# Issue order of the side work in the gate and up product of a SwiGLU layer: chunk loads and stores queued behind the unit loads

## The chip, the cores and the metric

The kernel runs on one core of one Trainium2 chip. Its time is the device time of one execution in microseconds. Three runs of the kernel before took 1671.94, 1673.28 and 1673.4 us; the median is 1673.28 us. The core's engines are called PE (matrix products), DVE (vector), ACT (scalar activation), POOL (GpSimd) and SP. SP computes nothing here: every transfer of this kernel is issued by SP, one after the other, and a transfer whose condition is not met holds all those written behind it.

## The reference, cut to what matters

One decoder layer with S = 1024 tokens and D = 1024 channels, all in float32. The first half (attention groups, a convolution branch, gates, an output projection, a LayerNorm) is not touched by the change. The second half is

```
def swiglu_ffn(x, w_gate, w_up, w_down):
    return (jax.nn.silu(x @ w_gate) * (x @ w_up)) @ w_down

x = layer_norm(alpha * x + swiglu_ffn(x, w_gate, w_up, w_down), ln2_g, ln2_b)
```

with 2816 hidden channels, 22 tiles of 128.

## The kernel before, in words

Each float32 product is made of three products of rounded halves: a matrix is split into `wh` (rounded, written by ACT, line 68) and `wl` (the rest, written by DVE, line 69), and PE adds `wh*xh + wl*xh + wh*xl`. On top of that the feed-forward uses a scheme with seven instead of eight half-size products (Strassen and Winograd), so sums of weight blocks and of activation blocks are needed.

**The tile loop** (`for f in range(NFF)`, line 1040). Tile f computes 128 hidden channels for all tokens. From tile 3 on it holds seven products of 12 matmuls, 84 in all; tiles 0 to 2 have 60, two products having been made early. The order on PE is B11 and B21 (gate), T2, T3, T1, then T4 (`t<-a22h` or `s<-a22h` in the trace), then B22. T4 is added into the same bank as T3, so PE may start it only when DVE has read T3's result (line 1072, `dve.tensor_add(u3, u2, pd)`).

**The weight units.** Each tile needs a gate unit g and an up unit u, 512 KB each, loaded by `fetch` (line 81, `raw<-wst`). While PE works on tile f, DVE and ACT prepare the weights of tile f+1: line 880 and 881 (`second`) form sums of u and g, line 885 and a split on ACT and DVE (`third`), then `fourth` and `fifth` (line 897). The two kinds of unit have separate pools: three buffers for g (`wraw`), two for u (`up2`). DVE runs its instructions in their written order, and line 880 for tile f+1 stands ahead of line 1072 for tile f.

**The chunks.** The down product, which follows the loop, also needs sums of its weights. They are made on the side in 22 chunks by `down_weights` (line 970): two loads of 256 KB (`tw<-wst`, lines 978 and 979), four POOL operations (lines 982 to 985) and, deferred to the next turn of the loop through the list `after`, two stores of 256 KB (`twd<-tw`, lines 988 and 989). Three buffers (`stage`) hold them. The loop text asks for one chunk in each tile from tile 3 on, and two in tiles 5, 9 and 13.

**The activation sums.** After each odd tile POOL forms four sums of the hidden activations (`down_sums`, lines 964 to 967, `h<-h`). Plain rows are stored at a tile's end (lines 1094, 1097 and 1098, `hdA<-h`), the sums through `after` (line 959, `hdS<-h`).

**What sets the order.** A scheduler places the instructions of each engine by when it reckons them ready, not by the order of the text. A chunk load depends on nothing but a free buffer, so the scheduler may put it far ahead of the place where the text has it.

Of the kernel before, what the change touches and what calls it, by code (L numbers as in the profile page):

```python
# [23 lines left out]
NEARLY = 3  # L24
# [17 lines left out]
def hybrid_layer(ctx: ExitStack, tc, wst, xT, xr, cosT, sinT, mask2, mask1, identc, convp, lnrows, out):  # L42
    nc = tc.nc
    pe, act, dve, sp = nc.tensor, nc.scalar, nc.vector, nc.sync
# [26 lines left out]
    state = {"raw": 0, "split": 0, "due": 0.0}  # L71
# [5 lines left out]
    def fetch(upto):  # L77
        while state["raw"] < min(upto, n_units):
            u = state["raw"]
            t = unit_pool[0](u).tile([P, 1024], F32, tag="raw", name="raw")  # L80
            sp.dma_start(t, wst[u])
            raws[u] = t
            state["raw"] += 1

    def prepare(upto):
        while state["split"] < min(upto, n_units):
            u = state["split"]
            fetch(u + 1)
            hi = wsplit.tile([P, 1024], F32R, tag="wh", name="wh")
            lo = wsplit.tile([P, 1024], F32R, tag="wl", name="wl")  # L90
            split(raws.pop(u), hi, lo)
            splits[u] = (hi, lo)
            state["split"] += 1
            fetch(u + 4)
# [11 lines left out]
    def take_into(w):  # L106
        u = taken[0]
        assert state["split"] == u
        taken[0] += 1
        fetch(u + 1)  # L110
        split(raws.pop(u), *w)
        state["split"] += 1
        fetch(u + 4)
        return w
# [788 lines left out]
    def product(ps, w, x, start=True, stop=True):  # L903
        n = 0
        for k in range(4):
            for a, b in three((w[0][:, k, :], w[1][:, k, :]), (x[0][:, k, :], x[1][:, k, :])):
                pe.matmul(ps, a, b, start=start and n == 0, stop=stop and n == 11,  # L907
                          skip_group_check=True)
                n += 1

    def bank(tag):
        return psum.tile([P, HALF], F32, tag=tag, name=tag)
# [8 lines left out]
    for n in range(NEARLY):  # L921
        t = stage.tile([P, S], F32, tag="sp", name="early")
# [27 lines left out]
    def half_tile():  # L950
        return gt6.tile([P, HALF], F32, tag="t", name="t")

    def row_tile():
        return h4.tile([P, S], F32, tag="h", name="h")
# [6 lines left out]
    def down_sums(k, u, v):  # L961

        eng = nc.gpsimd
        eng.tensor_add(v[:, RIGHT], v[:, RIGHT], u[:, RIGHT])
        eng.tensor_sub(u[:, RIGHT], u[:, LEFT], u[:, RIGHT])
        eng.tensor_sub(u[:, LEFT], v[:, RIGHT], u[:, LEFT])
        eng.tensor_sub(v[:, LEFT], v[:, LEFT], u[:, LEFT])
        after.append(lambda: spill_sums(k, u, v))

    def down_weights(k, e):  # L970

        t = stage.tile([P, 4, 256], F32, tag="sp", name="tw")
        cols = slice(e * 256, (e + 1) * 256)

        def rows(src, n):
            return src[n].rearrange("p (c x) -> p c x", c=2)[:, :, cols]

        sp.dma_start(t[:, 0:2], rows(wst, n_units + k))
        sp.dma_start(t[:, 2:4], rows(wst, n_units + NK + k))
        b11, b12, b21, b22 = (t[:, n] for n in range(4))  # L980
        eng = nc.gpsimd
        eng.tensor_sub(b12, b22, b12)
        eng.tensor_add(b11, b12, b11)
        eng.tensor_sub(b21, b21, b11)
        eng.tensor_sub(b22, b22, b11)  # L985

        def spill():
            sp.dma_start(rows(twd, k), t[:, 0:2])
            sp.dma_start(rows(twd, NK + k), t[:, 2:4])
        after.append(spill)  # L990

    chunks = deque((k, e) for k in range(NK) for e in range(2))
# [18 lines left out]
    def load_upto(n):  # L1011
        while dpos[0] < min(n, len(seq)):
            j, k = seq[dpos[0]]
            _, a, (kind, half), _, _ = DOWN[j]
            t = row_tile() if dpos[0] % 7 < 4 else wraw.tile([P, S], F32, tag="raw", name="raw")
            cols = slice(half * HALF, (half + 1) * HALF)
            b = wst[n_units + kind * NK + k] if kind < 2 else twd[(kind - 2) * NK + k]
            sp.dma_start(t[:, LEFT], hd[a][k])
            sp.dma_start(t[:, RIGHT], b[:, cols])
            draw[j, k] = t  # L1020
            dpos[0] += 1
# [12 lines left out]
    def start_down():  # L1034
        split_upto((0, 0), 1)
# [4 lines left out]
    for f in range(NFF):  # L1040
        last = f == NFF - 1
        todo, after = after, []
        for fn in todo:
            fn()
        if f >= NEARLY:
            for _ in range(2 if f in (5, 9, 13) else 1):
                if chunks:
                    down_weights(*chunks.popleft())
        V_, W = W, Weights()
        ta, tb_, tc_, td = sets[f % 2]  # L1050
        nxt = None if last else W
        if f < NEARLY:
            u2, sg1 = early[f]
            if nxt:
                nxt.first(f + 1 >= NEARLY)
        else:
            u2, sg1 = half_tile(), half_tile()
            pa = bank(ta)
            product(pa, V_.B11, A11, stop=False)
            act.activation(u2, pa, AF.Copy)  # L1060
            if nxt:
                nxt.first(f + 1 >= NEARLY)
        pb = bank(tb_)
        product(pb, V_.T2, S2)
        dve.tensor_add(u2, u2, pb)
        if f >= NEARLY:
            product(pa, V_.B21, A12, start=False)
            act.activation(sg1, pa, AF.Silu)
        u3, sg2 = half_tile(), half_tile()
        pd = bank(td)  # L1070
        product(pd, V_.T3, S3, stop=False)
        dve.tensor_add(u3, u2, pd)
        if last:
            load_upto(4)
        pc = bank(tc_)
        product(pc, V_.T1, S1, stop=False)
        dve.tensor_add(u3, u3, pc)
        if nxt:
            nxt.second()
        product(pd, V_.T4, a22, start=False)  # L1080
        dve.tensor_add(sg2, u2, pd)
        act.activation(sg2, sg2, AF.Silu)
        if nxt:
            nxt.third()
        else:
            start_down()
        product(pc, V_.B22, S4, start=False)
        dve.tensor_add(u2, u2, pc)
        ht = row_tile()
        dve.tensor_mul(ht[:, LEFT], sg1, u2)  # L1090
        dve.tensor_mul(ht[:, RIGHT], sg2, u3)
        k = FFN_ORDER[f] % NK
        if f % 2 == 0:
            sp.dma_start(hd["A11"][k], ht[:, LEFT])
            hrows.append(ht)
        else:
            sp.dma_start(hd["A12"][k], ht[:, LEFT])
            sp.dma_start(hd["A22"][k], ht[:, RIGHT])
            down_sums(k, hrows.pop(), ht)
        if nxt:  # L1100
            nxt.fourth()
            nxt.fifth()
# [203 lines left out]
```

## Time and profile before

| | before |
|---|---|
| median of three runs | 1673.28 us |
| the profiled execution | 1669.85 us |
| its span | 1668.0 us |
| PE busy | 1614.5 us, 97% of the span |
| DVE, ACT, POOL busy | 1034.5, 684.9, 161.9 us |
| mean granted TensorE clock | 0.984 |

The span is the stretch in which instructions ran; 1.85 us of the profiled execution lie around it. Times inside the span are counted from its start. The tile loop reaches from about 970 to 1449 us. A busy time is no proof that an engine is at its best: a matmul of this kernel is shown as 389 ns long, while the next one starts 227 ns after it, so the distance of starts is the measure. A granted clock of 1.0 is full speed, 2.4 GHz; half of it is 1.2 GHz.

### The profile page before, as it was taken

To read this page: it belongs to the slowest core of one execution; us is meant where nothing else is said; L and a number is where in the kernel's file an instruction comes from. 1 tells how busy PE (TensorE), PEld (TensorE's weight loads), DVE (VectorE), ACT (ScalarE), POOL (GpSimd) and SP (SyncE) were. 2 spreads that over 40 slices of the span, in tenths; PEclk is the share of its full clock that TensorE was granted. 3 is DMA by queue.
4 is the path that set the end of the run, shared out by engine and by line. 5 is a ranking of instruction groups with operands and counts; after the bars stand their busy time and mean duration, and the time that the engine had idled before them with its cause. 6 is when DMAs were issued, how large, how long until landed. Compare 5 with 4: busy or idle time off the path is not lost. (4 is left out here: it accounts for less than half of the span.)

```text
span 1668.0 us, 21325 instructions
## 1 busy us (share of the span) xinstructions
PE 1614.5 (97%) x8014; PEld 1316.0 (79%) x8014; DVE 1034.5 (62%) x1605; ACT 684.9 (41%) x1241; POOL 161.9 (10%) x148
## 2 busy tenths in 40 slices
PE   9999999999999999999999989867899999999998
PEld 7887788777887888887888868656788888888886
DVE  6944476553856942488756787454656666557685
ACT  5267743676345674334221142122232322344451
POOL 0000000000000000000000223555411112100000
PEclk9999999999999999999999999978999999999999
DMA  7111114111251124376725023766522332586761
GB/s 259 60 42 51 45 58 164 38 46 39 73 164 39 51 79 153 127 229 205 255 83 227 38 98 130 235 206 213 184 95 95 104 111 102 214 315 215 231 210 51
DMA packets 110812, 222.54 MB, mean 133 GB/s; under 512 B 14556, under 2 KB 39516, under 8 KB 110708
## 3 DMA queue, kind: packets, MB, share of 16 engines
q1 hardware_dynamic: 110708, 221.17, 39.4%
q8 instruction: 63, 1.03, 0.3%
q14 instruction: 41, 0.34, 0.1%
HBM read 159.81 MB, written 61.31 MB: 133 GB/s over the span
## 5 line engine op out<-in xcount | busy, mean ns | idle before, releaser
L68 ACT ACTIVATE wh<-raw 128x1024 fp32r<-128x1024 f32 (+1 forms) x192 | 192.4, 1002 | 442.2 <-PE mm L180 83.1
L69 DVE TENSOR_TENSOR wl<-raw,wh 128x1024 fp32r<-128x1024 f32 (+1 forms) x192 | 227.9, 1188 | 184.8 <-ACT wh L68 183.5
L180 PE MATMUL mm<-xh,wh 128*128 128x512 f32 x752 | 298.5, 397 | 0.0
L180 PE MATMUL mm<-xl,wh 128*128 128x512 f32 x752 | 293.2, 390 | 0.0
L180 PE MATMUL mm<-xh,wl 128*128 128x512 f32 x752 | 293.2, 390 | 0.0
L180 PEld LDWEIGHTS mm<-xh,wh 128*128 128x128 f32 x752 | 141.1, 188 | 39.3 <-issue 9.9
L180 PEld LDWEIGHTS mm<-xh,wl 128*128 128x128 f32 x752 | 141.2, 188 | 29.9
L180 PEld LDWEIGHTS mm<-xl,wh 128*128 128x128 f32 x752 | 141.3, 188 | 27.7
L508 DVE SCALAR_TENSOR_TENSOR acc<-u,cp,acc 128x1024 f32<-128x1024 f32 x120 | 153.9, 1282 | 3.3
L351 ACT ACTIVATE sw<-mm 32x512 f32<-32x512 f32 x192 | 113.3, 590 | 34.9 <-PE mm L180 16.5
L796 POOL TENSOR_TENSOR y<-y 128x512 f32<-128x512 f32 x3 | 6.5, 2167 | 956.9 <-DVE sc L618 947.6
L180 PE MATMUL mm<-wh,xh 128*128 128x512 f32 x232 | 91.5, 394 | 0.0
L180 PE MATMUL mm<-wh,xl 128*128 128x512 f32 x232 | 90.4, 390 | 0.0
L180 PE MATMUL mm<-wl,xh 128*128 128x512 f32 x232 | 90.3, 389 | 0.0
L353 DVE TENSOR_TENSOR tcs<-mm,cosF 128x512 f32<-128x512 f32 x48 | 33.2, 691 | 85.4 <-ACT sw L351 80.5
L69 DVE TENSOR_TENSOR wl<-h,wh 128x1024 fp32r<-128x1024 f32 x41 | 50.6, 1235 | 33.7 <-ACT wh L68 32.1
L68 ACT ACTIVATE wh<-h 128x1024 fp32r<-128x1024 f32 x41 | 43.5, 1061 | 63.7 <-PE s L1201 26.4
L382 DVE CUSTOM_DVE_ANT_0 pt<-s,m2t 128x256 f32<-128x256 f32 (+1 forms) x128 | 41.3, 378 | 35.4 <-PE s L418 35.4
L384 ACT ACTIVATE pt<-pt,stp 128x64 f32<-128x64 f32 (+2 forms) x128 | 49.9, 392 | 27.1 <-DVE stp L382 26.9
L907 PE MATMUL mm<-xh,wh 128*128 128x512 f32 x140 | 55.5, 398 | 4.4 <-ACT xh L785 4.4
L880 DVE TENSOR_TENSOR raw<-raw 128x512 f32<-128x512 f32 x22 | 16.6, 755 | 63.4 <-DMA raw<-wst 63.4
L907 PE MATMUL mm<-xl,wh 128*128 128x512 f32 x140 | 55.4, 396 | 0.0
(383 smaller groups left out, 3367.3 us busy)
## 6 DMA issues: line engine op xcount, KB each, us to landing
raw<-wst SPq DMA_DIRECT2D x121, 512.0 KB, 3.7
tw<-wst SPq DMA_DIRECT2D x44, 256.0 KB, 4.2
twd<-tw SPq DMA_DIRECT2D x44, 256.0 KB, 2.5
hdS<-h SPq DMA_DIRECT2D x44, 256.0 KB, 2.0
hdA<-h SPq DMA_DIRECT2D x33, 256.0 KB, 3.1
gd<-gt SPq DMA_DIRECT2D x16, 512.0 KB, 3.5
m<-gd SPq DMA_DIRECT2D x32, 256.0 KB, 5.1
h<-twd SPq DMA_DIRECT2D x25, 256.0 KB, 4.1
```

The lines of the kernel that those rows point to most:

```text
L68: act.activation(hi, src, AF.Copy)
L69: dve.tensor_sub(lo, src, hi.bitcast(F32))
L180: pe.matmul(ps, a, b, start=j == 0, stop=j == n - 1)
L351: act.activation(sw[32 * q:32 * q + 32, :], ps[32 * (q ^ 1):32 * (q ^ 1) + 32, :], AF.Copy)
L353: dve.tensor_mul(tcs, ps, cosF[:, cols])
L382: dve.tensor_tensor_reduce(out=pt, in0=s, in1=msk, scale=-0.125, scalar=BIG, op0=ALU.add, op1=ALU.min, accum_out=mneg)
L384: act.activation(pt, pt, AF.Exp, bias=mneg, scale=-1.0, accum_out=den)
L508: dve.scalar_tensor_tensor(acc, u[:, j:j + S], cp[:, c, j:j + 1], acc, op0=ALU.mult, op1=ALU.add)
L796: eng.tensor_add(v[:, RIGHT], v[:, RIGHT], v[:, LEFT])
L880: dve.tensor_sub(u[:, LEFT], u[:, RIGHT], u[:, LEFT])
L907: pe.matmul(ps, a, b, start=start and n == 0, stop=stop and n == 11, skip_group_check=True)
```

## The change

`fetch` keeps the instruction of the unit load that it issued last. In each turn of the tile loop, what the turn issues on SP of the deferred stores (`twd<-tw`, `hdS<-h`) and of the chunk loads (`tw<-wst`) is put behind that load in SP's order. This is a rule on the order of issue; no wait for the load's completion is added. Computation, sizes and buffers stay as they are. Lines behind 1042 have a number one higher in the changed kernel.

```
@@ -78,7 +78,7 @@
         while state["raw"] < min(upto, n_units):
             u = state["raw"]
             t = unit_pool[0](u).tile([P, 1024], F32, tag="raw", name="raw")
-            sp.dma_start(t, wst[u])
+            state["load"] = sp.dma_start(t, wst[u]).ins
             raws[u] = t
             state["raw"] += 1
 
@@ -1040,12 +1040,13 @@
     for f in range(NFF):
         last = f == NFF - 1
         todo, after = after, []
-        for fn in todo:
-            fn()
-        if f >= NEARLY:
-            for _ in range(2 if f in (5, 9, 13) else 1):
-                if chunks:
-                    down_weights(*chunks.popleft())
+        with tc.issue_after(state["load"]):
+            for fn in todo:
+                fn()
+            if f >= NEARLY:
+                for _ in range(2 if f in (5, 9, 13) else 1):
+                    if chunks:
+                        down_weights(*chunks.popleft())
         V_, W = W, Weights()
         ta, tb_, tc_, td = sets[f % 2]
         nxt = None if last else W
```

The order of instructions is the same on PE and on ACT. On DVE lines 880 and 885 change places in two tiles. SP and POOL change throughout the loop.

SP in tiles 2 and 3, before (`hdA_1_96` is the store at the end of tile 2; the second `raw` load is the u unit that tile 3 prepares for tile 4):

```order
L989 DMA twd_183<-tw 256x1x256
L978 DMA tw<-wst 128x2x256
L979 DMA tw<-wst 128x2x256
L978 DMA tw<-wst 128x2x256
L81 DMA raw<-wst 128x1024
L979 DMA tw<-wst 128x2x256
L988 DMA twd_173<-tw 256x1x256
L81 DMA raw<-wst 128x1024
L989 DMA twd_184<-tw 256x1x256
L1094 DMA hdA_1_96<-h 128x512
L988 DMA twd_173<-tw 256x1x256
```

The same place after:

```order
L81 DMA raw<-wst 128x1024 x2
L978 DMA tw<-wst 128x2x256
L1095 DMA hdA_1_96<-h 128x512
L979 DMA tw<-wst 128x2x256
L81 DMA raw<-wst 128x1024 x2
L1099 DMA hdA_1_118<-h 128x512
L1098 DMA hdA_1_107<-h 128x512
L988 DMA twd_172<-tw 256x1x256
L989 DMA twd_183<-tw 256x1x256
L959 DMA hdS_1_129<-h 128x512
```

Before, the chunk of rows 173 and 184, the third one, stands around the two unit loads, and a store that waits for POOL is directly ahead of the second. After, the two unit loads come as a pair ahead of the first chunk, and that chunk's stores stand behind the next pair. From there to the end of the loop one or two chunks stand between two pairs.

POOL at the same place, before, from the end of the second chunk on (each number names one buffer; `tw_8617` is the second chunk, `tw_8754` the third, `h_8346` and `h_8251` the activations of tiles 0 and 1):

```order
L985 TENSOR_TENSOR tw_8617<-tw_8617 128x256
L964 TENSOR_TENSOR h_8346<-h_8346,h_8251 128x512
L965 TENSOR_TENSOR h_8251<-h_8251 128x512
L966 TENSOR_TENSOR h_8251<-h_8346,h_8251 128x512
L967 TENSOR_TENSOR h_8346<-h_8346,h_8251 128x512
L982 TENSOR_TENSOR tw_8754<-tw_8754 128x256
```

and after (`tw_8471` is the first chunk, `h_8589` and `h_8454` the activations of tiles 2 and 3):

```order
L985 TENSOR_TENSOR tw_8471<-tw_8471 128x256
L964 TENSOR_TENSOR h_8589<-h_8589,h_8454 128x512
L965 TENSOR_TENSOR h_8454<-h_8454 128x512
L966 TENSOR_TENSOR h_8454<-h_8589,h_8454 128x512
L967 TENSOR_TENSOR h_8589<-h_8589,h_8454 128x512
L982 TENSOR_TENSOR tw_8617<-tw_8617 128x256
```

Before, two chunks stand ahead of the sums of tiles 0 and 1, and seven follow before the next sums. After, one chunk stands ahead of the sums of tiles 2 and 3, and three follow.

SP at the end of the loop, before (`hdA_9_104` is the store at the end of tile 18; `hdA_5_100` and the `wst` behind it are the sixth unit of the down product):

```order
L81 DMA raw<-wst 128x1024
L1094 DMA hdA_9_104<-h 128x512
L1018 DMA raw<-hdA_5_100 128x512
L1019 DMA raw<-wst 128x512
L1098 DMA hdA_9_126<-h 128x512
```

and after, where the sixth unit comes behind two more stores:

```order
L1095 DMA hdA_9_104<-h 128x512
L989 DMA twd_192<-tw 256x1x256
L978 DMA tw<-wst 128x2x256
L979 DMA tw<-wst 128x2x256
L978 DMA tw<-wst 128x2x256
L979 DMA tw<-wst 128x2x256
L978 DMA tw<-wst 128x2x256
L988 DMA twd_181<-tw 256x1x256
L989 DMA twd_192<-tw 256x1x256
L988 DMA twd_182<-tw 256x1x256
L989 DMA twd_193<-tw 256x1x256
L979 DMA tw<-wst 128x2x256
```

The last three chunks stand together there, between tile 18's store and the sixth unit of the down product.

## Rows read from the trace of the kernel before

**Rows 1.** Page, busy tenths of PE in 40 slices of the span.

```profile
PE   9999999999999999999999989867899999999998
```

**Rows 2.** Windows: stretch, length, busy us (x count) of PE, PEld, DVE, ACT, POOL; clock, DMA share, GB/s.

```profile
1040.00:1200.00 160.00, 125.87 (x501) 101.48 (x500) 79.58 (x91) 32.49 (x43) 89.36 (x94) 0.88 0.64 212
1200.00:1400.00 200.00, 200.00 (x884) 165.60 (x883) 125.45 (x160) 58.00 (x74) 27.41 (x20) 1.00 0.32 107
```

**Rows 3.** Timeline of PE: start, us, operation [idle before]; T4 of tiles 2, 3, 9 and 10.

```profile
1035.54 0.39 PE L907 MATMUL s<-a22h,wh 128*128 128x512 f32 x1
...
1060.19 0.80 PE L907 MATMUL t<-a22h,wh 128*128 128x512 f32 x1 [5.45 <-DVE t L1072]
...
1061.21 0.63 PE L907 MATMUL t<-a22h,wl 128*128 128x512 f32 x1
1061.64 0.63 PE L907 MATMUL t<-a22h,wh 128*128 128x512 f32 x1
...
1215.65 0.39 PE L907 MATMUL t<-a22h,wh 128*128 128x512 f32 x1
...
1234.69 0.39 PE L907 MATMUL s<-a22h,wh 128*128 128x512 f32 x1
```

**Rows 4.** Waits of PE from 1042 to 1177 us: total us, times, longest.

```profile
PE t L907 <- DVE t L1072: 17.2, 3, 7.3
PE s L907 <- DVE t L1072: 16.9, 2, 9.5
```

**Rows 5.** Timeline of DVE in tile 3.

```profile
1055.82 0.69 DVE L880 TENSOR_TENSOR raw<-raw 128x512 f32<-128x512 f32 x1 [8.76 <-DMA raw<-wst]
...
1059.46 0.68 DVE L1072 TENSOR_TENSOR t<-t,t 128x512 f32<-128x512 f32 x1
```

**Rows 6.** Timeline of SP's queue in tile 3.

```profile
1047.61 0.54 SPq L979 DMA_DIRECT2D tw<-wst  x1
1050.61 0.56 SPq L988 DMA_DIRECT2D twd<-tw  x1
1051.26 1.50 SPq L81 DMA_DIRECT2D raw<-wst  x1
```

**Rows 7.** Waits of SP's queue from 1042 to 1177 us.

```profile
SPq L988 <- POOL tw L983: 35.4, 15, 4.9
```

**Rows 8.** Timeline of SP's queue in tiles 9 to 12, two loads also alone.

```profile
1222.74 0.33 SPq L1097 DMA_DIRECT2D hdA<-h  x1
1226.95 4.43 SPq L959 DMA_DIRECT2D hdS<-h  x4
...
1239.73 0.33 SPq L81 DMA_DIRECT2D raw<-wst  x1
...
1241.78 0.33 SPq L1094 DMA_DIRECT2D hdA<-h  x1
1256.02 3.08 SPq L81 DMA_DIRECT2D raw<-wst  x2
```

**Rows 9.** Timeline of DVE in tile 11.

```profile
1243.53 0.69 DVE L880 TENSOR_TENSOR raw<-raw 128x512 f32<-128x512 f32 x1
...
1251.21 0.69 DVE L1072 TENSOR_TENSOR t<-t,t 128x512 f32<-128x512 f32 x1 [0.58 <-PE t L907]
```

**Rows 10.** The tile tw: operations, count, ns min/median/max, first and last start.

```profile
L978 SPq DMA_DIRECT2D tw<-wst x22: 539/592/632, 1016.9 to 1172.1; - x22
...
L982 POOL TENSOR_TENSOR tw<-tw x22: 723/737/1742, 1022.0 to 1179.8; 128x256 f32<-128x256 f32 x22
```

**Rows 11.** DVE line 1091 by groups, 1042 to 1177 us, then 1200 to 1390 us.

```profile
L1091 DVE TENSOR_TENSOR h<-t 128x512 f32<-128x512 f32 x5 | 6.2, 1231 | 0.0
...
L1091 DVE TENSOR_TENSOR h<-t 128x512 f32<-128x512 f32 x10 | 6.8, 684 | 0.0
```

**Rows 12.** End of the loop: SP's load of the sixth unit, PE's first matmul of the down product.

```profile
1408.33 0.33 SPq L1018 DMA_DIRECT2D raw<-hdA  x1
...
1449.57 0.39 PE L1201 MATMUL mm<-wh 128*128 128x512 f32 x1
```

## The prediction

> **What bounds the kernel now.** I read the page's slices first. PE is full nearly everywhere; the one long hole lies in slices 26 to 29, about 1040 to 1210 us, in the tile loop from tile 3 on (slice 24 is a short one ahead of the loop) [rows 1]. The windows put a size on it. From 1200 to 1400 us PE is busy without a break and gets the full clock; from 1040 to 1200 us it is busy 125.87 of 160 us and gets a mean clock of 0.88, so it loses twice: it stands still, and after standing still it runs slowly [rows 2]. Both stretches run the same tiles. The loop is bounded by PE in the second stretch and by something else in the first.
>
> What that is, the waits of PE say: five waits, 17.2 + 16.9 = 34.1 us, all at the start of product T4, all for DVE's line 1072 [rows 4]. DVE itself is not slow. In tile 3 it had stood 8.76 us ahead of line 880, waiting for a unit load, and line 1072 is written behind line 880 [rows 5]. The load in turn was not slow on the wire but issued late: on SP it stood behind a chunk store, which started at 1050.61 us, and the load's issue followed at 1051.26 [rows 6]. Chunk stores wait for POOL, and SP spent 35.4 us in 15 such waits in these tiles alone [rows 7]. The chain is POOL, chunk store, unit load, DVE line 880, DVE line 1072, PE. All 22 chunks pass here, their loads from 1016.9 to 1172.1 us [rows 10], and where they end the hole in PE ends.
>
> **The loss, counted from starts.** An undisturbed tile takes 1234.69 - 1215.65 = 19.04 us from T4 to T4 (84 matmuls, 227 ns each) [rows 3]. From T4 of tile 2 (1035.54) to T4 of tile 10 (1234.69) are eight tiles, which should take 152.3 us and took 199.15 [rows 3]. The loss is 46.8 us. Of it 34.1 us are the waits [rows 4]; the other 12.7 us, 2.5 us for each wait, are the slow start behind it: there two matmuls stand 1061.64 - 1061.21 = 0.43 us apart instead of 0.227, the pace at 1.2 GHz instead of 2.4 [rows 3].
>
> **Part 1: the unit loads no longer stand behind chunks that pile up.** How late may a u load be? In tile 11, which is undisturbed, the load is issued at 1239.73 [rows 8], line 880 runs at 1243.53 [rows 9], 3.8 us later, and T4 starts one tile after 1234.69, at 1253.73: 10.2 us after line 880. In tile 3 line 880 ran at 1055.82 [rows 5] and T4 followed at 1060.19 [rows 3]: 4.4 us are the least. So line 880 can be 10.2 - 4.4 = 5.8 us late at no cost. The first stall agrees: by the same distances the load was due 10.2 + 3.8 = 14.0 us ahead of T4's undisturbed start (1035.54 + 19.04 = 1054.58), at 1040.6; its issue at 1051.26 is 10.7 us late, its landing took 4.6 us instead of 3.8, and 10.7 + 0.8 - 5.8 = 5.7 us is what PE lost there (5.6). In the new order each pair of unit loads has at most one tile's stores and chunks ahead of it. The five stalls go: -46.8 us.
>
> **Part 2: what now stands ahead of a pair on SP.** Each tile gets one chunk, or two: two or four stores and two or four loads, at 0.56 and 0.59 us of issue [rows 6, 10]. Behind an odd tile, SP today waits from 1223.07 to 1226.95 for POOL's activation sums, 3.9 us, and issues the sums until 1231.38; the u load goes out at 1239.73, held by its buffer and not by SP [rows 8]. Four stores (2.2 us) fit into the first gap, and two loads (1.2 us) into the 8.3 us of the second. The stores wait for POOL operations on chunks whose loads went out a tile earlier. Behind an even tile SP has nothing to do from 1242.1 to 1256.02, 13.9 us [rows 8], and gets two to four loads, 2.4 us at most. So the u load leaves on time, with some 7 us in hand and 5.8 us more behind that. Cost 0. If that cover were gone, each tile would pay a stall and 2.5 us at the low clock; the chunks would then spread the old loss over 19 tiles, which is the slower rival below.
>
> **Part 3: POOL's work moves beside the rest of the loop.** Four operations of 0.74 us a chunk [rows 10] now run until the last tile. Where POOL was busy, DVE's line 1091 took 1231 instead of 684 ns, 0.55 us more [rows 11]. A tile has three DVE operations of that kind between the unit's landing and line 1072 (lines 880, 885, 69), so 1.6 us at most against 5.8 us in hand. Cost 0; the bound from below is 0 as well, since PE has no idle time left there to win.
>
> **Part 4: the traffic and the hand-over.** The bytes stay the same. The DMA share in an undisturbed tile is 0.32 against 0.64 in the disturbed ones [rows 2]; with a chunk in each tile it lies between, where a load should land in 4 us. At the end three chunks stand ahead of the sixth unit of the down product: five loads issued (3 us), a landing (4.6 us as above), three times four POOL operations (8.8 us), and for the load that waits for a buffer a second landing, some 21 us in all. Tile 18 ends three tiles ahead of the down product's start at 1449.57 [rows 12], at 1392.5, so that load goes out at about 1414, 6 us later than its 1408.33 [rows 12]. PE comes to the sixth unit five units of 12 matmuls later, at 1463. The lead of 55 us covers 6. Cost 0. The two swaps on DVE are of neighbours that both fit in the same slack: 0.
>
> **Sum.** Against the profiled execution: span 1668.0 - 46.8 = 1621.2, with the 1.85 us around it 1623.0. The profiled execution took 1669.85, 3.4 us less than the median of the three runs. Against the median: 1673.28 - 46.8 = 1626.5 us. Its own range is 1622 to 1632: 3 us for how runs differ, and 2 us for small waits.
>
> **Rivals.**
>
> *Stalls stay where two chunks meet (tiles 5, 9, 13).* There POOL works 5.9 us in a row beside line 69, which ends 0.6 us before line 1072 can start [rows 9, 10]. For it: in the crowded tiles DVE operations did grow by 0.55 us [rows 11]. Against it: such growth needs to eat 1.8 us, from line 1072's end at 1251.9 to T4 at 1253.73. Three stalls of 0.5 us with 2.5 us of slow clock each: 3 x 3.0 = 9 us, 1635. The Trainium skill, page SBUF — State Buffer, section "Who interferes with whom", says that a VectorE instruction with two SBUF inputs and a GpSimd instruction that reads SBUF exclude each other for a whole instruction, whichever began first. The trace agrees in size: the excess of 0.55 us is less than one POOL operation of 0.74 us. By that rule line 69 could pay one operation, and POOL in turn could pay up to one DVE operation for each of its own, which would lengthen the chunk that the next stores wait for. I give this rival 9%, where the slack alone would leave it 5%.
>
> *The hand-over pays.* The sums of tiles 18 and 19 wait behind the last three chunks, and a unit of the down product comes late: one gap of 5 us and 2.5 us of slow clock, 1634. The lead of 55 us speaks against it. 6%.
>
> *No change.* The units stay late because what holds them is a buffer or the wire, and the chunk stores only happened to stand there. For it: DMA shares of 0.64 in the bad stretch, 0.32 in the good one. Against it: SP's 35 us of waits for POOL [rows 7]. 1673. 2%.
>
> *Slower: the stall becomes regular.* The place is the row of a chunk's stores ahead of the activation sums, behind odd tiles, and of its loads ahead of the pair. If POOL, with chunks and sums now interleaved, finishes so late that the u load leaves later than its due time by more than 5.8 us in each of the 19 tiles with a chunk, each of them pays 0.5 + 2.5 = 3.0 us: 57 us given for 46.8 won, 1626.5 + 57 = 1683.5. It decides from 46.8 / 3.0 = 16 tiles on. For it: the old waits were just such waits, and now no tile is free of chunks. Against it: SP would have to be some 13 us later than today. 3%.
>
> **Chances and range.** The forecast has 80%, the two small rivals 15%, no change 2%, slower 3%. A run of this kernel can be told from no change at about 0.2%, 3.3 us. Faster is 80 + 15 = 95%. The range runs from 1621 to 1640: it holds the forecast with its spread and the two small rivals. What lies outside are no change, slower, and the cases in which a small rival is several times the size given, together under 2 in 10.
>
> **What would show it.** In the changed profile PE should have no wait for line 1072 inside the loop, T4 should follow T4 at 19.04 us in every tile from 3 to 21, and the granted clock should be 1.0 from 1000 us to the end of the loop. Line 880 should wait for a unit load by no more than fractions of a us. POOL's chunk operations should be spread to about 1370 us, and SP's waits for POOL should no longer stand ahead of a unit load that is due. The down product should start about 47 us earlier, at 1403, and take as long as before. I am wrong if the waits of PE for line 1072 are still there with the unit loads on time (then the chain is not the cause), or if they come back in the tiles that had none.

## The result and the profile after

| | before | after |
|---|---|---|
| median of four runs | 1673.34 us | 1622.0 us |
| lowest to highest | 1671.94 to 1675.63 | 1620.64 to 1622.49 |
| the profiled execution | 1669.85 us | 1620.64 us |
| its span | 1668.0 us | 1618.9 us |
| mean granted TensorE clock | 0.984 | 0.996 |

The change makes the kernel faster: 1622.0 / 1673.34 = 0.969 [0.967 to 0.971], 51.3 us less. The forecast was 46.8 us less, 1626.5, with 1622 to 1632 as its own range: the sign and the chain are right, the size is 4.5 us short, and 1622.0 is the very edge of that range.

The page's slices of PE, to be held against [rows 1], and a row of the tile `tw`, against [rows 10]:

```profile
PE   9999999999999999999999999999999999999997
```

```profile
L982 POOL TENSOR_TENSOR tw<-tw x22: 729/742/1727, 1045.1 to 1362.5; 128x256 f32<-128x256 f32 x22
```

The hole of PE is gone, and POOL's work on the chunks is spread to 1362.5 us, where it had ended at 1179.8. The two windows of [rows 2], of the kernel after (the columns are the same):

```profile
1040.00:1200.00 160.00, 160.00 (x707) 132.51 (x706) 104.14 (x126) 44.83 (x59) 60.30 (x56) 1.00 0.52 172
1200.00:1400.00 200.00, 200.00 (x884) 165.59 (x883) 128.56 (x152) 58.50 (x75) 75.10 (x68) 1.00 0.53 175
```

Both stretches now look alike: PE busy without a break at a clock of 1.00, and the traffic that stood at 0.64 and 0.32 is level at 0.52 and 0.53. T4 of tiles 2, 3 and 10 on PE, which answers to [rows 3]:

```profile
1033.65 0.39 PE L907 MATMUL s<-a22h,wh 128*128 128x512 f32 x1
...
1052.69 0.39 PE L907 MATMUL t<-a22h,wh 128*128 128x512 f32 x1
...
1185.97 0.39 PE L907 MATMUL s<-a22h,wh 128*128 128x512 f32 x1
```

1185.97 - 1033.65 = 152.32 us for eight tiles, 19.04 each. The loss in the loop is zero, and PE has no wait for line 1072 (now 1073) from 1035 us to the end of the loop. One link earlier on the chain, the wait of DVE's line 880 for a unit load, first before (1035 to 1220 us), then after (1035 to 1400 us):

```profile
DVE raw L880 <- DMA raw<-wst: 62.0, 6, 14.2
```

```profile
DVE raw L880 <- DMA raw<-wst: 0.2, 1, 0.2
```

And the link before that, SP's queue in tiles 3 and 4 of the kernel after, which answers to [rows 6, 8]:

```profile
1054.97 3.09 SPq L81 DMA_DIRECT2D raw<-wst  x2
1058.33 0.33 SPq L1099 DMA_DIRECT2D hdA<-h  x1
1059.77 0.33 SPq L1098 DMA_DIRECT2D hdA<-h  x1
1060.20 0.58 SPq L988 DMA_DIRECT2D twd<-tw  x1
1060.87 0.58 SPq L989 DMA_DIRECT2D twd<-tw  x1
1064.09 4.42 SPq L959 DMA_DIRECT2D hdS<-h  x4
1068.85 0.61 SPq L978 DMA_DIRECT2D tw<-wst  x1
1069.52 0.59 SPq L979 DMA_DIRECT2D tw<-wst  x1
1074.52 2.81 SPq L81 DMA_DIRECT2D raw<-wst  x2
```

Pair, stores, sums, one chunk's loads, pair: SP is through with the chunk at 1070.1 and the next pair goes out at 1074.52, held by its buffer. In the whole loop the pairs wait for DVE to free buffers. The wait of the chunk stores for POOL's line 983, 35.4 us in 15 pieces before [rows 7], is now (1035 to 1400 us):

```profile
SPq L81 <- DVE raw L897: 118.2, 16, 13.2
...
SPq L988 <- POOL tw L983: 8.2, 4, 4.5
```

That is one line of several. All waits of SP for POOL together are 62.5 us in this stretch, 48.2 of them ahead of the activation sums' stores (line 959). Before, they were 65.1 us from 1042 to 1177 us alone. SP still waits for POOL; what is gone is the unit load that was due behind such a wait.

At the end of the loop, the load of the sixth down unit and PE's first matmul of the down product, to be held against [rows 12]:

```profile
1367.83 0.56 SPq L1018 DMA_DIRECT2D raw<-hdA  x1
...
1400.85 0.39 PE L1202 MATMUL mm<-wh 128*128 128x512 f32 x1
```

The down product starts 48.7 us earlier (1449.57 before). With everything 48.7 us earlier the load would have gone out at 1359.6; it is 8.2 us late against that, where 6 were expected. PE waits for nothing there.

**Where the rest is.** Between the two profiled executions the spans differ by 49.1 us; 46.8 of it is the loop. Another 1.9 us lie ahead of T4 of tile 2, 1.7 of them before the loop, where the change alters nothing. At 791 us PE pauses for 1.45 us in both. Behind it the page's clock differs; the windows from 792 to 798 us, before and then after:

```profile
792.00:798.00 6.00, 5.98 (x19) 4.75 (x20) 5.23 (x8) 0.63 (x1) 0.00 (x0) 0.72 1.04 397
```

```profile
792.00:798.00 6.00, 6.00 (x26) 4.97 (x27) 5.23 (x8) 0.63 (x1) 0.00 (x0) 1.00 1.03 390
```

PE is busy all the time in both, but makes 19 against 26 matmuls: seven at 0.227 us are 1.6 us. A second profile of the kernel before (run 7) has the same pause and a clock of 1.00 behind it, and the profile of run 5, which is built on the kernel after, has 0.72. So this differs from execution to execution and is not the change.

### The profile page after: what moved, and what is told of

Same layout as the page of the kernel before. It is cut to its first block, busy times and chain, and to the rows that moved or that the text cites. A ratio compares the mean times of both kernels' runs of the same rounds, so it can differ in the third digit from the quotient of the medians.

```text
span 1618.9 us, 21299 instructions
## 1 busy us (share of the span) xinstructions
PE 1600.1 (99%) x8014; PEld 1307.6 (81%) x8014; DVE 1035.0 (64%) x1605; ACT 684.7 (42%) x1241; POOL 170.1 (11%) x148
## 4 chain that ended last, share of the span: by engine, by line
PE 95%; DVE 2%; DMA 1%; ACT 1%; issue 0%; SPq 0%; DVEq 0%; ACTq 0%
PE mm L180 44%; PE mm L907 10%; PE t L907 7%; PE s L907 7%; PE mm L1202 6%; PE s L180 4%; PE s L1202 3%; PE t L1202 3%; PE s L418 2%; PE pv L907 2%; PE pv L464 2%; PE t L438 1%; PE pv L1202 1%; PE pv L180 1%; PE pv L456 1%; DMA m<-ctd 1%
## 5 line engine op out<-in xcount | busy, mean ns | idle before, releaser
L69 DVE TENSOR_TENSOR wl<-raw,wh 128x1024 fp32r<-128x1024 f32 (+1 forms) x192 | 231.2, 1206 | 198.6 <-ACT wh L68 197.7
L180 PE MATMUL mm<-xh,wl 128*128 128x512 f32 x752 | 293.2, 390 | 0.0
L68 ACT ACTIVATE wh<-h 128x1024 fp32r<-128x1024 f32 x41 | 43.5, 1060 | 63.0 <-PE s L1202 24.9
L382 DVE CUSTOM_DVE_ANT_0 pt<-s,m2t 128x256 f32<-128x256 f32 (+1 forms) x128 | 41.3, 379 | 35.4 <-PE s L418 35.3
L907 PE MATMUL mm<-xh,wl 128*128 128x512 f32 x140 | 54.9, 392 | 0.0
```

The costliest lines, as they stand in the source:

```text
L68: act.activation(hi, src, AF.Copy)
L69: dve.tensor_sub(lo, src, hi.bitcast(F32))
L180: pe.matmul(ps, a, b, start=j == 0, stop=j == n - 1)
L382: dve.tensor_tensor_reduce(out=pt, in0=s, in1=msk, scale=-0.125, scalar=BIG, op0=ALU.add, op1=ALU.min, accum_out=mneg)
```

## The experiments

Theory in all of them: the loss is the chain POOL, chunk store on SP, unit load, DVE line 880, line 1072, PE; whatever keeps the chunks from standing ahead of a due unit load gains all of it.

**1. The rule for the chunks alone** (edit against the kernel after). The deferred stores, the chunks' among them, are left to the scheduler; the chunk loads are ordered.

```diff
+        for fn in todo:
+            fn()
         with tc.issue_after(state["load"]):
-            for fn in todo:
-                fn()
```

> Only the chunk loads are put behind the last unit load; the chunk stores and the stores of the activation sums keep the scheduler's own order, and fall in the same tile as their loads, ahead of the next pair of unit loads. Theory (a unit load is late only when several chunks' waits pile up ahead of it): a chunk's round (issue, landing, four POOL operations) takes about 8 us of the 14 us that SP has to spare, so no stall, 1622 +- 3 us. Rival (the stores are what blocks, and they must be ruled themselves): stalls of some us in each tile, 1640 us or more.

Measured: 1622.1 us (1621.83 to 1622.45), ratio 0.971 [0.968 to 0.973]. T4 of tiles 2 and 10 are 152.32 us apart (1034.64 and 1186.96), as after. The wait of the chunk stores on SP, 1035 to 1400 us:

```profile
SPq L988 <- POOL tw L983: 60.0, 22, 5.3
```

The stores do stand ahead of the next pair here, and every chunk's first store waits for POOL. SP waits longer for them than in the kernel before (60.0 us against 35.4 [rows 7], or 43.5 from 1035 to 1450 us), and PE has no wait for line 1073. So a store that waits for POOL ahead of a pair is not the loss by itself: the wait of one tile's chunks fits into the gap between two pairs, that of a pile does not.

**2. The rule for the stores alone** (edit against the kernel after): the chunks are moved out of the `with`.

```diff
-            if f >= NEARLY:
+        if f >= NEARLY:
...
```

> Only the deferred stores are put behind the last unit load; the chunk loads may go as early as a buffer is free. Theory: three buffers hold the loads back as soon as the stores are spread, so the pile cannot form, 1622 +- 3 us. Rival (the loads' early place is what blocks): 1640 us or more.

Measured: 1621.75 us (1620.56 to 1622.97), 0.970 [0.968 to 0.973]; T4 of tiles 2 and 10 again 152.32 us apart (1033.33 and 1185.65). So either half does it. Three buffers hold the chunks: a chunk load can run ahead only as far as the stores free buffers, and a store only follows a load. To hold back either is enough to keep the pile from forming.

**3. The chunks on another queue** (edit against the kernel before). If only the position on SP matters, taking the chunks off SP should also gain everything.

```diff
-        sp.dma_start(t[:, 0:2], rows(wst, n_units + k))
-        sp.dma_start(t[:, 2:4], rows(wst, n_units + NK + k))
+        nc.gpsimd.dma_start(t[:, 0:2], rows(wst, n_units + k))
+        nc.gpsimd.dma_start(t[:, 2:4], rows(wst, n_units + NK + k))
...
-            sp.dma_start(rows(twd, k), t[:, 0:2])
-            sp.dma_start(rows(twd, NK + k), t[:, 2:4])
+            nc.gpsimd.dma_start(rows(twd, k), t[:, 0:2])
+            nc.gpsimd.dma_start(rows(twd, NK + k), t[:, 2:4])
```

> The kernel before, with the four transfers of each chunk issued by POOL's queue and not by SP's, and no rule on the order: the chunks may crowd into the first tiles as before. Theory (SP's queue, in which stores that wait for POOL stand ahead of unit loads): the five stalls go, 1622 to 1628 us. Rival (crowding: the wire, or POOL beside DVE, is what makes the tiles slow): the loss stays in tiles 3 to 8, 1655 us or more.

Measured: 1805.83 us (1804.28 to 1806.34), 1.080 [1.078 to 1.083]. The theory missed. By its size the time falls to the rival (1655 us or more), but the traces show another reason than crowding. The waits of PE (1040 to 1400 us), of SP's queue and of POOL (both 1040 to 1310 us):

```profile
PE t L907 <- DVE t L1072: 177.0, 4, 83.9
```

```profile
SPq L959 <- POOL h L964: 195.7, 3, 97.7
```

```profile
POOL tw L979 <- issue: 46.9, 18, 6.1
POOL tw L978 <- issue: 45.4, 20, 3.6
POOL twd L989 <- issue: 35.7, 18, 2.6
POOL twd L988 <- issue: 14.2, 11, 2.6
```

Ahead of its transfers POOL stands still for 142 us in 67 pieces, 1.3 to 2.6 us each on the mean, with nothing that the profile shows to wait for ("issue"). POOL does its work in order, so the activation sums (line 964) stand behind a pile of chunks; their stores, line 959, wait for them on SP, and the unit loads stand behind those stores. SP's queue in one of PE's four stalls:

```profile
1080.18 0.33 SPq L1097 DMA_DIRECT2D hdA<-h  x1
1158.75 6.05 SPq L959 DMA_DIRECT2D hdS<-h  x4
1164.92 0.84 SPq L81 DMA_DIRECT2D raw<-wst  x2
```

SP issues nothing for 78 us, then the store, then the pair. That is the chain again, with another store in the middle. The DMA engines are busy only 0.25 of the time from 1100 to 1160 us, so the wire is not what the loads wait for.

**4. Without POOL's sums of the chunks** (edit against the kernel after): what does POOL's spread work still cost?

```diff
-        eng.tensor_sub(b12, b22, b12)
-        eng.tensor_add(b11, b12, b11)
-        eng.tensor_sub(b21, b21, b11)
-        eng.tensor_sub(b22, b22, b11)
```

> The changed kernel without the four POOL operations of each chunk: the chunks are loaded and stored unsummed. Theory (they cost nothing in the changed kernel, part 3): 1622 +- 2 us. Rival (POOL beside DVE costs small delays): 3 us or more faster than the changed kernel.

Measured: 1620.61 us (1619.8 to 1621.57), 0.970 [0.967 to 0.972], 1.4 us under the kernel after, about the spread of its runs; as a ratio to the kernel before, measured along with each, it is 0.970 against 0.969, so no gain shows. T4 to T4 of tiles 2 and 10 is 152.32 us here too. DVE's line that [rows 11] shows (now 1092), 1042 to 1177 us, in the kernel after and then in this one:

```profile
L1092 DVE TENSOR_TENSOR h<-t 128x512 f32<-128x512 f32 x7 | 6.4, 916 | 0.0
```

```profile
L1088 DVE TENSOR_TENSOR h<-t 128x512 f32<-128x512 f32 x7 | 4.8, 684 | 0.0
```

Beside POOL the mean grows by 232 ns, without POOL it is back at 684. The operations do grow, as the Trainium skill has it (page SBUF — State Buffer, section "Who interferes with whom"). They do not always: in run 1, with POOL's work at other times, the mean of this line is 684 ns too. The growth stays within the slack, and PE does not see it.

**5. Each chunk made twice** (edit against the kernel after; the second goes to spare memory). Twice the loads, POOL operations and stores, at the same places: if crowding of wire or POOL costs anything, or if the slack on SP is smaller than worked out, it shows.

```diff
                 for _ in range(2 if f in (5, 9, 13) else 1):
                     if chunks:
+                        down_weights(*chunks[0], into=spare)
                         down_weights(*chunks.popleft())
```

> The changed kernel with every chunk made twice, the copy going to spare memory that nobody reads: two chunks in a tile, four in tiles 5, 9 and 13. Theory (12 to 13 us in hand behind odd tiles, more behind even ones): two chunks in a tile cost nothing and four perhaps a stall of some us; 1622 to 1632 us. Rival (the stall becomes regular as soon as a second chunk stands in each tile): 3 us in each of 19 tiles, 1675 us or more.

Measured: 1643.86 us (1642.17 to 1650.6), 0.982 [0.981 to 0.984], above what I expected. The profile is of the slowest of the four runs, 1650.6 us, so its stalls may be larger than those of the others. The window from 1236 to 1290 us, tiles 12 to 15, in which two chunks stand in a tile and four in tile 13:

```profile
1236.00:1290.00 54.00, 54.00 (x240) 44.72 (x239) 38.62 (x41) 14.54 (x19) 37.09 (x36) 1.00 0.71 236
```

The DMA share is 0.71, above that of the bad stretch of before (0.64 in [rows 2], 0.68 from 1042 to 1177 us alone), POOL is busy 37.09 of 54 us (before: 89.36 of 160), and PE is full at the whole clock. In this stretch the crowd by itself costs PE nothing. But the waits of PE, 1035 to 1440 us (in this kernel line 1072 is 1076):

```profile
PE t L908 <- DVE t L1076: 21.5, 4, 13.1
```

Four stalls: 1.71, 4.90 and 1.77 us in tiles 7, 11 and 15, two tiles behind those with four chunks, and 13.10 us in tile 21. In the second of them, on SP and on DVE:

```profile
1199.74 0.61 SPq L981 DMA_DIRECT2D tw<-wst  x1
1200.46 1.01 SPq L82 DMA_DIRECT2D raw<-wst  x2
```

```profile
1209.41 1.13 DVE L881 TENSOR_TENSOR raw<-raw 128x512 f32<-128x512 f32 x1 [9.64 <-DMA raw<-wst]
```

T4 came at 1214.22, where one tile after the last T4 (1190.13) would have been 1209.17. The due time of part 1, 14.0 us ahead of that, is 1195.2; the second load went out at 1201.1, 5.9 us late, behind chunk loads, and line 881 ran 8.3 us later instead of 3.8. 5.9 + 4.5 - 5.8 = 4.6 us, and 5.05 were lost: the sum of part 1 holds within half a us in a kernel that it was not made from. Nearly half of the lateness is the slower landing, at a DMA share of 0.83 from 1200 to 1210 us: here the crowd does take a part. In tile 21, ACT, and the load of the down unit on SP:

```profile
1418.08 1.06 ACT L69 ACTIVATE wh<-h 128x1024 fp32r<-128x1024 f32 x1 [19.02 <-DMA h<-wst]
```

```profile
1411.76 0.45 SPq L1020 DMA_DIRECT2D h<-hdA  x1
```

Here the down units' loads are late behind the last six chunks. ACT waits 19.02 us for one, DVE for ACT, and line 1076 stands behind both: the hand-over stalls not where PE needs the unit, but in the last tile of the loop, where ACT and DVE prepare it.

**6. Each chunk made three times** (as 5, with a third copy).

```diff
                     if chunks:
+                        down_weights(*chunks[0], into=spare)
+                        down_weights(*chunks[0], into=spare2)
                         down_weights(*chunks.popleft())
```

> The changed kernel with every chunk made three times, two copies going to spare memory: three chunks in a tile, six in tiles 5, 9 and 13, where the kernel before had between four and five a tile in its bad stretch. Theory: the slack is used up; stalls in tiles 5, 9 and 13 at least, PE waiting for line 1072 or its like behind late unit loads, 1630 to 1670 us. Rival (density of chunks does not matter once the order is ruled): 1622 +- 3 us.

Measured: 1711.48 us (1709.88 to 1713.88), 1.023 [1.022 to 1.025], slower than before and far above what I expected. Waits of PE, of SP's queue and of DVE, 1035 to 1500 us:

```profile
PE t L909 <- DVE t L1078: 76.6, 8, 20.3
```

```profile
SPq L991 <- POOL tw L986: 77.9, 50, 6.0
SPq L992 <- POOL tw L988: 58.9, 49, 2.3
```

```profile
DVE raw L882 <- DMA raw<-wst: 90.3, 12, 16.5
```

The eight stalls lie in the odd tiles from 7 to 21, 1.91 to 20.31 us each; the four of about 13 us and more are two tiles behind those with six chunks, and in tile 21. In tile 7 the unit load went out at 1134.36, 19.8 us after its due time by part 1, and landed 5.9 us later, so most of the lateness is on SP. This is the slower rival of the prediction, chunk stores that wait for POOL ahead of the pairs, though in every second tile and not in each. It begins, as far as runs 5 and 6 tell, between two and three chunks in a tile, and the change asks for one.

**7. The kernel before once more**, for its profile alone.

> The kernel before once more, for the spread of its loss. Theory: five waits of PE for line 1072 again, 34 +- 4 us, and 46.8 +- 4 us lost between T4 of tile 2 and T4 of tile 10; the 1.45 us pause at 791 us may or may not be followed by a slow stretch, worth about 2 us. Rival (the loss in that stretch is the same to the tenth, and the spread of the times comes from elsewhere): 46.8 +- 0.3 us.

Measured: 1666.81 us, span 1665.0. T4 of tiles 2 and 10, and the waits of PE from 1042 to 1177 us:

```profile
1033.44 0.39 PE L907 MATMUL s<-a22h,wh 128*128 128x512 f32 x1
...
1232.16 0.39 PE L907 MATMUL s<-a22h,wh 128*128 128x512 f32 x1
```

```profile
PE t L907 <- DVE t L1072: 17.4, 3, 7.3
PE s L907 <- DVE t L1072: 16.8, 2, 9.8
```

198.72 - 152.32 = 46.4 us lost, with 34.2 us of waits: the loss repeats within 0.4 us [rows 3, 4]. The clock from 792 to 798 us was 1.00 here.

**8. The unit loads on another queue** (edit against the kernel before): inside the loop ACT issues them, and the chunks stay on SP in the old order.

```diff
-            sp.dma_start(t, wst[u])
+            (act if "loop" in state else sp).dma_start(t, wst[u])
```

> The kernel before, with the unit loads of the tile loop issued by ACT's queue and not by SP's, and no rule on the order: on SP the chunks may pile up as much as before or more, at the same bytes. Theory (the loss is the unit load's place behind POOL-waiting stores in one queue): PE's waits for line 1072 go, 1622 to 1632 us, unless the activations' stores, now alone behind the pile on SP, hold their buffers so long that DVE waits for one of those. Rival (crowding of the wire, or POOL beside DVE): the loss stays, 1655 us or more. It is the try that the chunks on POOL's queue failed to be, since there POOL's sums, and with them SP, came to stand behind the pile.

Measured: 1678.55 us (1676.0 to 1682.33, ten runs), 1.003 [1.002 to 1.004]. The gain does not come, as the rival had it, and yet PE's waits for line 1072 are gone, as the theory had it. Waits of PE and of ACT, 1035 to 1250 us:

```profile
PE mm L907 <- ACT t L1061: 26.1, 2, 14.2
PE s L907 <- ACT t L1061: 20.8, 2, 14.2
```

```profile
ACT t L1083 <- DMA tw<-wst: 37.1, 3, 14.1
...
ACT t L1061 <- DMA tw<-wst: 21.4, 3, 9.4
```

ACT's queue and ACT in the first such wait:

```profile
1075.16 0.34 ACTq L81 DMA_DIRECT2D raw<-wst  x1
1075.54 0.63 ACT L1083 ACTIVATE t<-t 128x512 f32<-128x512 f32 x1 [13.30 <-DMA tw<-wst]
```

ACT stands still for 13.30 us until it has issued the unit load, and what released it was a transfer of a chunk on SP. Line 1083 itself reads no chunk, so it is the load ahead of it that waited. That a load on ACT's queue waits for earlier transfers of SP's is how the profile reads; why it should, no run shows. The block moved from SP to ACT, and this run can't say what free unit loads alone would gain.

## Why the prediction was right, and where it was short

**What bounds the kernel.** Right: the hole was PE's wait for line 1072 through a unit load issued late. Shown by what takes it away (the change, runs 1 and 2) and by what builds it again: run 3 with another store in the chunk store's place, run 6 with more chunks. Run 5 rules out that the crowd on the wire or POOL's work alone does it. One link is longer than the chain says. In the first stall (tile 3) POOL had itself stood idle, until the chunk's load landed:

```profile
1049.02 0.74 POOL L982 TENSOR_TENSOR tw<-tw 128x256 f32<-128x256 f32 x1 [5.70 <-DMA tw<-wst]
```

From 1042 to 1177 us POOL waited 28.4 us in 7 such pieces. A chunk store thus waits for its chunk's whole round (load, landing, two POOL operations), and a faster POOL alone would shorten only a part of that.

**The loss counted from starts.** Right to 0.1 us: 46.8 us, the loop's loss, is what the loop gave back. Counting waits alone would have given 34.1; the 12.7 us of half clock behind the waits came back with them.

**Part 1.** Right, and the due time (line 880 may be 5.8 us late) also gave the size of a stall in run 5. The 3.8 us that it calls a landing are the way from issue to line 880: the unit loads of that tile landed in 3.1 to 3.2 us, and DVE was still at other work. The sums use only differences, so they stand.

**Part 2.** The cost, 0, is right. The reserve behind it, "some 7 us in hand and 5.8 us more", was too large for what it was used for. It counted SP's issue time, took the stores' wait for POOL as over by then, and let a unit load land in 4 us (8.3 in run 5). In tile 5 of the kernel after the unit landed with DVE already asking for it, by 0.2 us. One chunk more per tile is free, four in a tile cost up to 4.9 us two tiles later, and three in each tile with six in three of them make the kernel slower than before. The true reserve is about one chunk per tile. It did not touch the result, since the change asks for no more.

**Part 3.** Right: 0 within 1.4 us (run 4).

**Part 4.** The cost, 0, is right, and the sixth unit is 8.2 us late instead of 6. The argument was not: "the lead of 55 us" is PE's, and for the sixth unit, but the first who needs a down unit is ACT, in tile 21, and DVE's line 1072 stands behind it. There, in the kernel after:

```profile
1388.41 1.06 ACT L68 ACTIVATE wh<-h 128x1024 fp32r<-128x1024 f32 x1 [3.08 <-DMA h<-wst]
```

ACT waited 3.08 us for this unit (1.72 before), and PE lost nothing. By the gaps that follow (0.52 us on ACT, 0.58 on DVE, 1.83 from the end of line 1073 to T4), my estimate is that it could have come 2.9 us later (4.3 before), not 55. Run 5 stalls there for 13.1 us with six chunks where the change has three. So the hand-over rival had the right place, and the reason given against it does not hold.

**The sum.** Here lies the 4.5 us. "Against the median: 1673.28 - 46.8" carries a loss from one profiled execution to the other runs. Against its own execution the sum gave 1623.0, and 1620.64 came: 1.9 of these 2.4 us lie ahead of T4 of tile 2, most of it the half clock at 791 us, and the other half us behind the loop and around the span. For the median the difference is 51.3 us. The profiled executions of the kernel before, 1669.85 and 1666.81, lie 3.5 and 6.5 us under its median, that of the kernel after 1.4 us. So the other runs lose some more in the kernel before than the profiled one shows. Their mean granted clocks point the same way: among all runs of the kernel before on record the fastest, 1664.89 us, had 0.987 and the slowest, 1677.04 us, 0.982. In which stretch the longer ones run slower, no trace tells, and this remains open. 2 to 3 us hang on it.

**The rivals.** No change: fell. Stalls where two chunks meet: none in the kernel after; at twice the chunks they come at 1.71 to 4.90 us, where 0.5 was estimated, and the one that was followed up (tile 11) comes through late issue and slow landing rather than through growing DVE operations. The regular stall: real at three chunks a tile, in every second tile. None of the other versions is better than the kernel after: the loop has no loss left, and runs 1, 2 and 4 lie within 1.4 us of it.

## What to carry to other kernels

Where one queue issues everything, a small transfer that waits for its own data holds back every urgent one written behind it: look in the queue's own rows for what stands ahead of the late load, and give the urgent load the earlier place. Not the sum of such waits decides, but whether a due load stands behind them (run 1: more waiting, no loss). Count the loss from starts of equal work (T4 to T4), since the waits alone leave out the slow clock behind them, here a quarter of it. Before moving side work to another queue, ask what stands in order behind the issuing engine: on POOL and on ACT the same block came back, on POOL with five times PE's waits (177.0 us against 34.1).

## What the runs showed of the hardware

Ahead of a transfer that POOL issues, POOL stood up to 6.1 us with nothing that the profile shows to wait for, and the row of the transfer itself is 0.7 us (run 3); on SP the rows of the same transfers are 0.54 to 0.61 us on the median (kernel before). A pause of PE is not always followed by half clock: the 1.45 us at 791 us were in one profile of the kernel before and were not in the other. The five waits of the loop, 4 to 10 us each, were followed by half clock in both, with 2.5 us lost behind each.
